# Linear attention's state updates as single fp32 products of unsplit keys and values, in one burst of alternating row halves

## The chip, the core and the metric

The kernel runs on one core of a Trainium2 chip. The core has a matrix engine (TensorE, here PE; its weight loads are listed as PEld), a vector engine (VectorE, DVE), a scalar engine (ScalarE, ACT), GpSimd (POOL) and SyncE (SP). SP and POOL issue most of the DMAs. Each engine works through its own queue in program order and waits on semaphores that the others raise. The metric is the device time of one execution, in microseconds; the figures quoted are medians of several runs, and the profile is of one more execution.

## The reference, cut to what matters

Two layers of a hybrid encoder, over 512 frames of width 2048. In each layer one input projection feeds a gated linear attention (GLA) with four heads and a chunked softmax attention with eight; both are normalised, gated, concatenated and mapped by one output projection. The change is in the linear attention, in its state updates `U`:

```
def gla_chunk_causal(q, k, v, log_a):
    ...
    L = jnp.cumsum(log_a.astype(jnp.float32).reshape(B, nc, CHUNK, H, DK), axis=2)
    L_end = L[:, :, -1]
    k_dec = kf * jnp.exp(L_end[:, :, None] - L)
    U = jnp.einsum('bnchk,bnchv->bnhkv', k_dec, vf)
    A = jnp.exp(L_end)
    def step(state, inp):
        a, u = inp
        new = a[..., None] * state + u
        return new, new
    ...
    o = jnp.einsum('bnchk,bnhkv->bnchv', qf, states)
```

A chunk is 64 frames, there are eight of them; a head's keys are 128 wide (DK) and its values 256 (DV). So `U` is, for each of the four heads and eight chunks, a product of a 64 x 128 by a 64 x 256 matrix: the 64 frames are the rows of the array that are summed over, and the result is 128 x 256.

## The kernel before

**Precision.** The large projections are computed from split operands: a value x is stored as a rounded part hi (type fp32r) and the rest lo = x - hi, and a product is the sum of three fp32r products, hi·hi, hi·lo and lo·hi. `split` (L107) makes hi with a cast on ACT (L108) and lo with a subtraction on DVE (L109); `split_scaled` (L111) does the same with a factor (L112, L113). Some smaller products use fp32 operands as they are: the attention's mixing (L920), transposes, and the reading of the GLA states (L1124).

**The main stream.** `std_gemm` (products at L341) and `fast_gemm` (L417 with features as rows, L427 otherwise) run through the weight blocks in a fixed list of jobs. For each job SP fetches a 512 KB block (`raw` or `H`, L156), ACT casts its hi part (`wh`, L218), DVE makes its lo part (`wl`, L223), and PE multiplies. Blocks are prepared some jobs ahead, in rings of four buffers (`wl`: three). Beside this stream, generators in a list `tasks` are advanced by `pump` after each job (`Pace`), so that the products of the attention heads, the GLA heads and the like stand between main products. The order in which each engine's queue is written is then settled by a scheduler that simulates the program; it can put main products into the middle of what the code writes as one group.

**The GLA part of a layer.** After the softmax heads, `fast_gemm` with the block pair GK, GQ calls `kq_consume` for each of four token tiles of keys and of queries. A key tile is multiplied by its decay and split into `kdh` and `kdl` (slots g8, g11, g14, g15). The pair GV0, GV1 calls `gv_consume`: value tiles are split into `gvh` and `gvl`, one pair of slots for each j (two heads) and each half of the frames p. When both halves of a j are there, `gla_heads` is started: it makes a `Unit` for each of two heads and two halves of the frames, eight units a layer. A unit does

- `outer` (products at L1090): for each of its four chunks (tile tt, half cc of the tile's 128 rows) the three products kh·vh, kh·vl, kl·vh, 64 rows by 256 columns, into `ps_u[cc]`, a PSUM bank of the pool of four that all `ax` tiles share. That is 12 products a unit. The half cc = 0 lies on the array's rows 0 to 63, cc = 1 on rows 64 to 127;
- `states` (L1109, L1111): four steps on DVE, each chunk's state from the one before and `ps_u`;
- `read` (L1124): four fp32 products of the queries with the states, each to one half (64 columns) of the array;
- `norm`, `gate`, and later `turn` (transposes at L1152, and the result's split and its store `fg`, L1167).

After the two GV blocks come the output projection's blocks (`std_gemm`, L341). `output_sums` loads pieces of the heads' results (`fa`, L655, and `fg`, L659), adds and splits them and stores sums (L629), and token rows of x are loaded on POOL's queue (L497), behind the last norm.

Of the kernel before, what the change touches and what calls it, by code (L numbers as in the profile page):

```python
# [8 lines left out]
F32R = mybir.dt.float32r  # L9
# [25 lines left out]
def hybrid_trunk(  # L35
# [674 lines left out]
    def layer(l):  # L710
# [319 lines left out]
        kdh, kdl, gqT = [], [], []  # L1030
# [13 lines left out]
        def kq_consume(j, h, t, src, comb):  # L1044
            z = settled(src, comb)
            if j:
                if not gqT:
                    until(lambda: 6 in heads_done)
                    gqT.extend(slot(tag, [2, 512]) for tag in ("g12", "g13"))
                tasks.insert(0, transpose_q(2 * h + t, z))  # L1050
                return
            if not kdh:
# [17 lines left out]
        class Unit:  # L1070
            def __init__(self, h, p, gvh, gvl, prev):
                self.h, self.p, self.gvh, self.gvl = h, p, gvh, gvl
                self.st = slot(f"g{9 + p}", [4, 256])
                self.prev = prev.st[:, 3, :] if p else None

            def outer(self):
# [4 lines left out]
                for tt in range(2):  # L1081
                    ops = []
                    for cc in range(2):
                        r = slice(cc * 64, (cc + 1) * 64)
                        kh, kl = kdh[p][r, tt, hk], kdl[p][r, tt, hk]
                        vh, vl = self.gvh[p][r, tt, hv], self.gvl[p][r, tt, hv]
                        ops.append(((kh, vh), (kh, vl), (kl, vh)))
                    for i in range(3):
                        for cc in range(2):
                            nc.tensor.matmul(  # L1090
                                self.ps_u[cc][:, tt * 256 : (tt + 1) * 256], ops[cc][i][0], ops[cc][i][1],
                                start=(i == 0), stop=(i == 2),
                            )
# [77 lines left out]
        def gla_heads(j, gvh, gvl):  # L1171
            units = []

            def new(k):
                h, p = 2 * j + k // 2, k % 2
                units.append(Unit(h, p, gvh, gvl, units[-1] if p else None))
                units[-1].outer()
# [30 lines left out]
        gvh, gvl = {}, {}  # L1208
        GV = {1: ("g4", "g5", "g6", "g7"), 0: ("g0", "g1", "g2", "g3")}
# [16 lines left out]
        def gv_consume(j, h, t, src, comb):  # L1226
            z = settled(src, comb)
            if (j, h) not in gvh:
                until(lambda: 4 in heads_done)
                gvh[j, h] = slot(GV[j][h], [2, 512], F32R)  # L1230
                gvl[j, h] = slot(GV[j][2 + h], [2, 512], F32R)
            if comb is None:
                split_scaled(gvh[j, h][:, t, :], gvl[j, h][:, t, :], src, inv_rms(l, 2 * h + t))
            else:
                split(gvh[j, h][:, t, :], gvl[j, h][:, t, :], z)
            if h and t:
                heads = gla_heads(j, [gvh[j, p] for p in range(2)], [gvl[j, p] for p in range(2)])
# [172 lines left out]
```

## Time and profile before

| what | value |
|---|---|
| median of 3 runs | 1637.59 us (1635.76 to 1638.52) |
| the profiled execution, its own time | 1637.15 us |
| its span, first to last instruction | 1635.2 us |
| mean granted TensorE clock | 0.999 |
| HBM, read and written | 395.83 MB and 71.06 MB, 286 GB/s over the span |
| weight blocks, SP, 512 KB each | 319 + 56, median 5.8 and 5.2 us from issue to landing |

In a list of instruction groups each row has line, engine, operation, what is written from what, shapes, count, then busy time in us, mean duration of one in ns, and the engine's idle time just before them with what ended it. In the timeline a row is start and duration in us and what ran, neighbours of one kind merged with their count. A matmul's duration holds the time until its results are out, so that the next starts before its end: what a product costs in a stream is read from start to start. A layer's GLA units stand at about 593 to 673 us of the span in the first layer and 1407 to 1487 us in the second.

### The profile page before, as it was taken

The numbers are of one execution on the slowest core, as the hardware profiler recorded it, in microseconds if no ns is written. First come the engines' busy times: TensorE is split into PE (matmuls) and PEld (weight loads), VectorE is DVE, ScalarE is ACT, GpSimd is POOL, SyncE is SP. The second block draws the span as 40 slices with busy tenths as digits, with TensorE's granted clock in tenths as the row PEclk, the third lists the DMA queues.
The fourth block names the chain that finished last, engine by engine and source line by source line (L and its number), as shares of the span: only waits on it lengthen the run. The fifth ranks groups of instructions, "written<-read, shape, count | busy, mean of one in ns | idle before, by whom it ended". The sixth has DMA issues, their size and how long they took to land.

```text
span 1635.2 us, 24844 instructions
## 1 busy us (share of the span) xinstructions
PE 1625.8 (99%) x8990; PEld 1392.6 (85%) x8990; DVE 1228.0 (75%) x1587; ACT 904.6 (55%) x1516; POOL 169.9 (10%) x259
## 2 busy tenths in 40 slices
PE   9999999999999999999999999999999999999998
PEld 7888889999978877788888888899999888777886
DVE  7567776877877886778886676768778778866887
ACT  8444544556676644555783445445566665445553
POOL 1210000001101201310122000000001012013100
PEclk9999999999999999999999999999999999999999
DMA  9979786858868696898789697968588676969986
GB/s 374 360 280 322 283 313 227 304 181 311 291 196 283 208 378 233 308 364 315 276 303 388 228 332 268 321 221 304 187 312 274 218 265 232 355 225 332 376 307 233
DMA packets 150778, 469.59 MB, mean 287 GB/s; under 512 B 16428, under 2 KB 35892, under 8 KB 150656
## 3 DMA queue, kind: packets, MB, share of 16 engines
q1 hardware_dynamic: 128064, 389.69, 68.1%
q0 software_dynamic: 22016, 77.37, 12.0%
q8 instruction: 71, 1.16, 0.3%
q10 hardware_dynamic: 576, 0.95, 0.2%
q14 instruction: 51, 0.42, 0.1%
HBM read 395.83 MB, written 71.06 MB: 286 GB/s over the span
## 4 chain that ended last, share of the span: by engine, by line
PE 99%; DMA 0%; DVE 0%; ACT 0%; SPq 0%; DVEq 0%; POOLq 0%; issue 0%
PE mm L427 46%; PE mm L341 22%; PE mm L417 20%; PE ax L920 2%; PE ax L1090 1%; PE ax L427 1%; PE ax L903 1%; PE ax L1124 1%; PE ax L745 1%; PE ax L882 1%; PE ax L883 1%; PE ax L881 1%; PE ax L1152 0%; PE ax L569 0%; PE ax L951 0%; DMA raw<-in_w_dram 0%
## 5 line engine op out<-in xcount | busy, mean ns | idle before, releaser
L427 PE MATMUL mm<-wh,sa 128*128 128x512 f32 x1536 | 485.1, 391 | 0.0
L218 ACT CAST wh<-raw 128x1024 fp32r<-128x1024 f32 x255 | 269.1, 1057 | 255.7 <-PE mm L427 115.8
L223 DVE TENSOR_TENSOR wl<-raw,wh 128x1024 fp32r<-128x1024 f32 (+1 forms) x257 | 312.3, 1217 | 125.5 <-PE mm L427 44.1
L218 ACT CAST wh<-H 128x1024 fp32r<-128x1024 f32 x224 | 235.3, 1053 | 217.6 <-PE mm L427 109.9
L223 DVE TENSOR_TENSOR wl<-H,wh 128x1024 fp32r<-128x1024 f32 x224 | 273.1, 1222 | 106.6 <-PE mm L427 46.4
L427 PEld LDWEIGHTS mm<-wh,sa 128*128 128x128 f32 x1536 | 287.9, 188 | 62.2 <-issue 1.5
L427 PE MATMUL mm<-wl,sa 128*128 128x512 f32 x768 | 299.9, 390 | 0.0
L417 PE MATMUL mm<-sa,wh 128*128 128x256 f32 x1280 | 237.3, 286 | 0.0
L417 PEld LDWEIGHTS mm<-sa,wh 128*128 128x128 f32 x1280 | 199.9, 191 | 0.3
L427 PE MATMUL mm<-wh,a 128*128 128x512 f32 x576 | 185.7, 393 | 0.0
L417 PE MATMUL mm<-sa,wl 128*128 128x256 f32 x640 | 180.6, 283 | 0.0
L427 PEld LDWEIGHTS mm<-wl,sa 128*128 128x128 f32 x768 | 144.3, 188 | 30.3
L341 PE MATMUL mm<-wh,a 128*128 128x512 f32 x512 | 167.4, 394 | 0.1
L207 DVE TENSOR_TENSOR H<-H,raw 128x1024 f32<-128x1024 f32 x120 | 145.9, 1220 | 3.5 <-DMA raw<-in_w_dram 1.8
L465 POOL TENSOR_TENSOR sm<-sm,mhalf 128x4 f32<-128x4 f32 (+2 forms) x40 | 60.6, 1514 | 777.7 <-DVE sm L936 550.8
L427 PEld LDWEIGHTS mm<-wh,a 128*128 128x128 f32 x576 | 107.9, 188 | 23.2 <-issue 0.8
L417 PEld LDWEIGHTS mm<-sa,wl 128*128 128x128 f32 x640 | 122.3, 191 | 0.1
L341 PEld LDWEIGHTS mm<-wh,a 128*128 128x128 f32 x512 | 96.0, 188 | 21.1 <-ACT wh L215 0.5
L427 PE MATMUL mm<-wl,a 128*128 128x512 f32 x288 | 113.0, 392 | 0.0
L341 PE MATMUL mm<-wl,a 128*128 128x512 f32 x256 | 100.1, 392 | 0.0
L417 PE MATMUL mm<-a,wh 128*128 128x256 f32 x512 | 94.9, 285 | 0.0
L341 PE MATMUL mm<-wh,sa 128*128 128x512 f32 x256 | 85.9, 394 | 0.0
(208 smaller groups left out, 2332.9 us busy)
## 6 DMA issues: line engine op xcount, KB each, us to landing
raw<-in_w_dram SPq DMA_DIRECT2D x319, 512.0 KB, 5.8
sa<-S SPq DMA_DIRECT2D x192, 512.0 KB, 4.7
H<-in_w_dram SPq DMA_DIRECT2D x56, 512.0 KB, 5.2
sa<-A SPq DMA_DIRECT2D x48, 512.0 KB, 6.1
S<-g POOLq DMA_DIRECT2D x32, 512.0 KB, 7.6
oS<-g POOLq DMA_DIRECT2D x32, 512.0 KB, 6.3
sa<-oS SPq DMA_DIRECT2D x32, 512.0 KB, 5.2
sg<-t POOLq DMA_DIRECT2D x32, 256.0 KB, 6.1
```

The lines of the kernel that those rows point to most:

```text
L207: nc.vector.tensor_tensor(out=h, in0=h, in1=r, op=ALU.add)
L218: last_cast[0] = nc.scalar.copy(self.wh, src).ins
L223: last_low[0] = nc.vector.tensor_tensor(out=self.wl[:, kk, :], in0=self.src[:, kk, :], in1=self.wh[:, kk, :].bitcast(F32), op=ALU.subtract ...
L341: mm = nc.tensor.matmul(pss[o], a[:, part, t], rhs[:, kk, :], start=(i == 0 and kk == 0 and m == 0), stop=(i == n - 1 and kk == 1 and m == 2),
L417: nc.tensor.matmul(dst, lhs[:, kk, f], a[:, part, tok], start=(fresh and kk == 0 and m == 0 and ft % 2 == 0), stop=(c == c_last and kk == ...
L427: nc.tensor.matmul(out_ps[t], a[:, part, tok], rhs[:, kk, :], start=(fresh and kk == 0 and m == 0), stop=(c == c_last and kk == 1 and m == ...
L465: return nc.gpsimd.tensor_tensor(out=out_r, in0=v, in1=mhalf[:, : v.shape[-1]], op=ALU.pow).ins
L745: nc.tensor.matmul(ps[0:96, half * 256 : (half + 1) * 256], wga[kt // 10][:, kt % 10, :], op[:, i, (kt % 2) * 256 : (kt % 2 + 1) * 256], s ...
L881: nc.tensor.matmul(ps[:, :n], self.qh[:, t], self.kh[:, :n], start=True, stop=False)
L882: nc.tensor.matmul(ps[:, :n], self.qh[:, t], self.kl[:, :n], start=False, stop=False)
L883: nc.tensor.matmul(ps[:, :n], self.ql[:, t], self.kh[:, :n], start=False, stop=True)
L920: nc.tensor.matmul(o, self.pt[i][:, j * P : (j + 1) * P], av[hd // 4, j // 2][:, j % 2, (hd % 4) * P : (hd % 4 + 1) * P], start=(j == 0), ...
```

## The change

Keys and values are no longer split: `kq_consume` writes the decayed keys into fp32 slots `kd`, `gv_consume` writes the values into fp32 slots `gv`, and `outer` makes one fp32 product for each chunk where it made three fp32r ones. The four products of a unit alternate between the row halves (cc = 1, 0, 1, 0), each with an edge to the one before, so that the scheduler keeps their order. A one-column memset on DVE of `ps_u[0]` stands before them. The slots g14, g15, g6, g7, g2 and g3 are no longer used for this. `Unit`, `gla_heads` and their callers take `gv` in place of `gvh` and `gvl`.

```
         def kq_consume(j, h, t, src, comb):
-            z = settled(src, comb)
             if j:
+                z = settled(src, comb)
...
-                kdh.extend(slot(tag, [2, 512], F32R) for tag in ("g8", "g11"))
-                kdl.extend(slot(tag, [2, 512], F32R) for tag in ("g14", "g15"))
+                kd.extend(slot(tag, [2, 512]) for tag in ("g8", "g11"))
+            dst = kd[h][:, t, :]
             if comb is None:
-                kd, z = z, t2()
                 nc.vector.scalar_tensor_tensor(
-                    out=z, in0=kd, scalar=inv_rms(l, 2 * h + t), in1=decay[h][:, t, :], op0=ALU.mult, op1=ALU.mult
+                    out=dst, in0=src, scalar=inv_rms(l, 2 * h + t), in1=decay[h][:, t, :], op0=ALU.mult, op1=ALU.mult
                 )
             else:
-                nc.vector.tensor_tensor(out=z, in0=z, in1=decay[h][:, t, :], op=ALU.mult)
-            split(kdh[h][:, t, :], kdl[h][:, t, :], z)
+                z = settled(src, comb)
+                nc.vector.tensor_tensor(out=dst, in0=z, in1=decay[h][:, t, :], op=ALU.mult)
...
                 self.ps_u = [aux(), aux()]
-                for tt in range(2):
-                    ops = []
-                    for cc in range(2):
+                nc.vector.memset(self.ps_u[0][:, 0:1], 0.0)
+                mm = None
+                for tt in (1, 0):
+                    for cc in (1, 0):
                         r = slice(cc * 64, (cc + 1) * 64)
-                        kh, kl = kdh[p][r, tt, hk], kdl[p][r, tt, hk]
-                        vh, vl = self.gvh[p][r, tt, hv], self.gvl[p][r, tt, hv]
-                        ops.append(((kh, vh), (kh, vl), (kl, vh)))
-                    for i in range(3):
-                        for cc in range(2):
-                            nc.tensor.matmul(
-                                self.ps_u[cc][:, tt * 256 : (tt + 1) * 256], ops[cc][i][0], ops[cc][i][1],
-                                start=(i == 0), stop=(i == 2),
-                            )
+                        with tc.issue_after(mm) if mm else nullcontext():
+                            mm = nc.tensor.matmul(
+                                self.ps_u[cc][:, tt * 256 : (tt + 1) * 256], kd[p][r, tt, hk], self.gv[p][r, tt, hv],
+                                start=True, stop=True,
+                            ).ins
...
-        GV = {1: ("g4", "g5", "g6", "g7"), 0: ("g0", "g1", "g2", "g3")}
+        GV = {1: ("g4", "g5"), 0: ("g0", "g1")}
...
-            z = settled(src, comb)
-            if (j, h) not in gvh:
+            if (j, h) not in gv:
                 until(lambda: 4 in heads_done)
-                gvh[j, h] = slot(GV[j][h], [2, 512], F32R)
-                gvl[j, h] = slot(GV[j][2 + h], [2, 512], F32R)
+                gv[j, h] = slot(GV[j][h], [2, 512])
+            dst = gv[j, h][:, t, :]
             if comb is None:
-                split_scaled(gvh[j, h][:, t, :], gvl[j, h][:, t, :], src, inv_rms(l, 2 * h + t))
+                nc.scalar.activation(dst, src, AF.Copy, scale=inv_rms(l, 2 * h + t))
             else:
-                split(gvh[j, h][:, t, :], gvl[j, h][:, t, :], z)
+                comb(dst)
```

In the changed program the line numbers past the new code are smaller by four: the outer products are L1086 (before L1090), the reads L1120 (before L1124), the memset is L1080.

Where these products stand in PE's queue is settled by the scheduler. The rows below are a place in the first layer, of the third unit (head 3, first half of the frames), before the change. A row is line, operation, what it writes from what (with the buffers' numbers) and the shape; `ax_6307` and `ax_6308` are the two banks `ps_u[0]` and `ps_u[1]`, that is the two row halves, and `ax_6321` is the read of the unit before. The six products of the other half (`ax_6307`) stand six main products earlier, in a row too.

```order
L427 MATMUL mm_5724<-wl_6205,a_55_470 128x512
L1090 MATMUL ax_6308<-g_1142_6092,g_1028_5572 128x256
L1090 MATMUL ax_6308<-g_1143_6093,g_1028_5572 128x256
L1090 MATMUL ax_6308<-g_1142_6092,g_1030_5574 128x256
L1090 MATMUL ax_6308<-g_1142_6092,g_1028_5572 128x256
L1090 MATMUL ax_6308<-g_1143_6093,g_1028_5572 128x256
L1090 MATMUL ax_6308<-g_1142_6092,g_1030_5574 128x256
L1124 MATMUL ax_6321<-g_1172_6233,g_977_5335 64x256 x4
L427 MATMUL mm_5724<-wh_6179,a_55_470 128x512
```

The same unit in the changed program; `ax_6267` and `ax_6268` are its two banks.

```order
L427 MATMUL mm_5712<-wl_6179,a_55_470 128x512
L1086 MATMUL ax_6268<-g_1137_6078,g_1027_5570 128x256
L1086 MATMUL ax_6267<-g_1137_6078,g_1027_5570 128x256
L1086 MATMUL ax_6268<-g_1137_6078,g_1027_5570 128x256
L1086 MATMUL ax_6267<-g_1137_6078,g_1027_5570 128x256
L1120 MATMUL ax_6274<-g_1162_6200,g_977_5335 64x256 x4
L427 MATMUL mm_5712<-wh_6160,a_55_470 128x512
```

A layer's 96 outer products in 17 groups, some of both halves, some of one half alone, become 32 in eight groups of four, each alternating. Groups of outer products and of reads that stand directly side by side are five a layer before and four after; one read that was in two pieces is in one.

SP's queue changes too. This is a place about 100 us after a layer's GLA units begin, in the first layer before the change: weight fetches (L156), and the loads of heads' results for the output sums (L655, L659).

```order
L156 DMA raw_7142<-in_w_dram 128x1024
L655 DMA t_1395_7226<-fa_173 128x2x256
L156 DMA raw_7165<-in_w_dram 128x1024
L156 DMA raw_7295<-in_w_dram 128x1024
L659 DMA t_1396_7227<-fg_181 128x512
L156 DMA raw_7329<-in_w_dram 128x1024
```

And the same place in the changed program.

```order
L156 DMA raw_7050<-in_w_dram 128x1024
L655 DMA t_1381_7134<-fa_173 128x2x256
L659 DMA t_1382_7135<-fg_181 128x512
L156 DMA raw_7073<-in_w_dram 128x1024
L156 DMA raw_7203<-in_w_dram 128x1024
L655 DMA t_1383_7136<-fa_173 128x2x256
```

The load L659 has moved ahead of two weight fetches. It waits until the store of `fg` that used its buffer before has landed (on the first layer's timeline, the store issued by POOL at 692.34 us).

More of the change, by code (lines that the diff above doesn't have):

```diff
@@ L1169, in turn, with gla_heads @@
                 og[p, h] = op
-        def gla_heads(j, gvh, gvl):
+        def gla_heads(j, gv):
             units = []
@@ L1226, in gv_consume @@
         def gv_consume(j, h, t, src, comb):
[L1227 to L1228 removed]
+            if (j, h) not in gv:
                 until(lambda: 4 in heads_done)
[L1230 to L1231 removed]
+                gv[j, h] = slot(GV[j][h], [2, 512])
+            dst = gv[j, h][:, t, :]
             if comb is None:
[L1233 removed]
+                nc.scalar.activation(dst, src, AF.Copy, scale=inv_rms(l, 2 * h + t))
             else:
[L1235 removed]
+                comb(dst)
             if h and t:
[L1237 removed]
+                heads = gla_heads(j, [gv[j, p] for p in range(2)])
                 tasks.append(heads if j else beside(heads, early_sums(), 3))
```

12 lines of the change are left out of this document (6 added, 6 removed).

## The prediction

> **What bounds the kernel now.** The page comes first: the span, the busy shares and the chain that ended last.
>
> ```profile
> span 1635.2 us, 24844 instructions
> PE 1625.8 (99%) x8990; PEld 1392.6 (85%) x8990; DVE 1228.0 (75%) x1587; ACT 904.6 (55%) x1516; POOL 169.9 (10%) x259
> PE 99%; DMA 0%; DVE 0%; ACT 0%; SPq 0%; DVEq 0%; POOLq 0%; issue 0%
> ```
>
> The matrix engine is the chain, so the end moves by what the change does to PE's own sequence, and by any wait it puts into it. A busy PE is not yet a PE at its peak, so next I read the two lines concerned (shortest, median and longest ns of a weight load and of a product, then rows*columns of the array), and the list of what the weight loads wait for.
>
> ```profile
> L1090 PEld LDWEIGHTS ax<-g,g x192: 182/184/188, 593.3 to 1478.1; 64*128 64x128 f32 x192
> L1090 PE MATMUL ax<-g,g x192: 271/278/386, 593.3 to 1478.2; 64*128 64x256 f32 x192
> ...
> L1124 PEld LDWEIGHTS ax<-g,g x128: 132/136/137, 610.5 to 1487.1; 128*64 128x64 f32 x128
> L1124 PE MATMUL ax<-g,g x128: 379/379/430, 610.5 to 1487.3; 128*64 128x256 f32 x128
> ...
> PEld ax L1090 <- issue: 8.1, 24, 0.4
> ```
>
> L1090 is the outer products (64 rows of the array), L1124 the state reads (64 columns). The program has 64 reads and the trace 128 records: an unsplit fp32 product runs as two records. The fp32r products of L1090 have one each. In 24 places the weight loader stands 0.34 us (8.1/24) in front of an outer product for nothing that the profile shows. To see why, I went through the timeline at such places; columns are start and duration in us, then what ran.
>
> ```profile
> 592.79 0.39 PE L427 MATMUL mm<-wl,sa 128*128 128x512 f32 x1
> 593.01 0.39 PE L427 MATMUL mm<-wh,sa 128*128 128x512 f32 x1
> 593.33 0.38 PE L1090 MATMUL ax<-g,g 64*128 64x256 f32 x2
> 593.65 0.49 PE L427 MATMUL mm<-wh,sa 128*128 128x512 f32 x1
> 593.98 0.39 PE L427 MATMUL mm<-wl,sa 128*128 128x512 f32 x1
> ...
> 625.12 0.39 PE L427 MATMUL mm<-wh,sa 128*128 128x512 f32 x1
> 625.43 0.97 PE L1090 MATMUL ax<-g,g 64*128 64x256 f32 x6
> 626.33 0.50 PE L427 MATMUL mm<-wh,sa 128*128 128x512 f32 x1
> 626.67 0.40 PE L427 MATMUL mm<-wl,sa 128*128 128x512 f32 x1
> ...
> 663.14 0.39 PE L341 MATMUL mm<-wl,a 128*128 128x512 f32 x1
> 663.46 0.99 PE L1090 MATMUL ax<-g,g 64*128 64x256 f32 x12
> 664.38 0.50 PE L341 MATMUL mm<-wh,a 128*128 128x512 f32 x1
> 664.71 0.39 PE L341 MATMUL mm<-wh,sa 128*128 128x512 f32 x1
> ```
>
> Start to start, main products follow each other every 0.22 to 0.23 us (I use 0.227). Into the burst the step is 0.32, out of it 0.32, and the first step after it 0.33. So every excursion from full-array products to row halves and back has a fixed price, which I call the switch. An excursion costs (next main start less last main start less 0.227) + (first step after it less 0.227):
> - 2 products, one on each half: 0.64 - 0.227 + 0.33 - 0.227 = 0.52.
> - 6 products, all on one half (the order shown with the change tells which): 1.21 + 0.34 - 0.454 = 1.10.
> - 12 products, 6 on each half: 1.24 + 0.33 - 0.454 = 1.12.
>
> Twelve cost what six do: **the two row halves run side by side**, and they did although the order issues four of one half, then four of the other. What counts is the slots, the products on the fuller half: 0.40 + 0.117 per slot (from 0.52 at one and 1.10 at six).
>
> **The change part by part.** *PE, removed.* Following L1090 through order and timeline, a layer has 17 excursions with 1, 2, 1, 3, 1, 5, 6, 6, 6, 6, 1, 6, 6, 6, 6, 6, 6 slots, 74 together. Standing alone they cost 17 x 0.40 + 74 x 0.117 = 15.5 us. The eight reads stand in nine excursions; one whole read, and one that touches a burst:
>
> ```profile
> 633.36 0.40 PE L427 MATMUL mm<-wl,sa 128*128 128x512 f32 x1
> 633.69 1.08 PE L1124 MATMUL ax<-g,g 128*64 128x256 f32 x8
> 634.70 0.50 PE L427 MATMUL mm<-wh,sa 128*128 128x512 f32 x1
> 635.04 0.40 PE L341 MATMUL mm<-wh,a 128*128 128x512 f32 x1
> ...
> 616.12 0.40 PE L427 MATMUL mm<-wl,a 128*128 128x512 f32 x1
> 616.45 0.97 PE L1090 MATMUL ax<-g,g 64*128 64x256 f32 x6
> 617.36 1.08 PE L1124 MATMUL ax<-g,g 128*64 128x256 f32 x8
> 618.37 0.50 PE L427 MATMUL mm<-wh,a 128*128 128x512 f32 x1
> 618.71 0.40 PE L427 MATMUL mm<-wh,sa 128*128 128x512 f32 x1
> ```
>
> A read costs 1.34 + 0.34 - 0.454 = 1.23. Together with the burst it is 2.25 + 0.34 - 0.454 = 2.14, against 1.10 + 1.23 = 2.33 apart: a join saves 0.19. The ninth excursion, one product of a split read, I put at 0.8 (a read less half its 0.7 of later slots). Reads: 8 x 1.23 + 0.8 = 10.6; the order joins five times, -0.95. Before: 15.5 + 10.6 - 0.95 = 25.1 us a layer.
>
> *PE, added.* A new burst has four fp32 products, two on each row half, two records each: four slots a half. No row shows a 64-row fp32 product. The nearest is the read, which also has four fp32 products of 256 columns, on two column halves: its eight records take 1.08, the last alone 0.38 (379 ns), so 0.70 for the three slots before it, some 0.21 to 0.27 each. Hence the read's 1.23, plus 0.05 because the first weight load, which nothing hides, brings 128 columns and not 64 (medians 184 and 136 ns): 1.28. Bounds: 1.10, the six fp32r slots, and 1.28 + 4 x 0.21 = 2.12 with no overlap; I take 1.28, the read being the same arithmetic. After: 8 x 1.28 + 8 x 1.23 - 4 joins x 0.19 = 19.3 a layer. **Saved: 2 x (25.1 - 19.3) = 11.6 us.** All other products are the same in number and shape.
>
> A sentence apart: the Trainium skill, FP8 and Floating Point Precision, "TensorE Precision Notes", gives true FP32 four passes through the array, so one product would stream more than the three it replaces (64 x 4 against 192 passes of 256 columns), and as an estimate, at half of the read's 0.21 us slot for a pass and with no overlap on either side, the change would lose 64 x 0.105 = 6.7 us. The trace agrees with the passes (a read's record lasts 0.10 longer than an fp32r product of as many columns, and there are two) and adds the overlap and the switches, which that count leaves out.
>
> *DVE and ACT.* The splits go: ten casts on ACT and twelve vector operations on DVE a layer. Eight memsets come.
>
> ```profile
> L109 DVE TENSOR_TENSOR g<-t,g 128x512 fp32r<-128x512 f32 x12 | 8.2, 685 | 0.1
> L223 DVE TENSOR_TENSOR wl<-raw,wh 128x1024 fp32r<-128x1024 f32 x16 | 19.6, 1223 | 9.0 <-PE mm L341 3.9 <-PE mm L427 3.6 <-ACT t L1134 1.0
> L862 DVE MEMSET bias<- 64x64 f32 x16 | 1.8, 112 | 6.2 <-DMA bias<-in_rel_dram 6.1
> ```
>
> These are DVE groups (the first two from 580 to 670 us alone, the third from the whole run): count, busy time, mean ns, idle before. Freed on DVE: about 12 x 0.69 = 8.2 us a layer; the memset of a column costs at most the 0.11 of a wider one. I price both at nothing for the end, since PE covers them. The new wait is the point: in four of a layer's eight bursts, by the order with its waits, the second product waits for DVE, with all main products queued behind it. Bounds: 0, and one L223 ahead of each memset, 16 x 1.22 = 19.6 us. I take 0, because here DVE idles 9.0 us before its L223, mostly for PE: it runs ahead.
>
> *What is late next.* PE reaches the stage after the heads 5.8 us earlier in each layer. That stage is fed by DMA. The stretches first (their last two figures are the DMA engines' share and GB/s), then the timeline:
>
> ```profile
> 655.00:660.00 5.00, 5.00 (x28) 3.51 (x28) 4.12 (x10) 0.82 (x2) 0.71 (x1) 1.00 0.01 4
> 700.00:710.00 10.00, 10.00 (x46) 8.06 (x44) 5.25 (x8) 3.37 (x6) 0.54 (x1) 1.00 1.04 402
> ```
>
> ```profile
> 709.93 0.19 PEld L341 LDWEIGHTS mm<-wl,a 128*128 128x128 f32 x1 [0.31 <-DVE wl L223]
> ...
> 692.34 0.55 POOL L1167 DMA_DIRECT2D fg<-t  x1 [0.83 <-DMA g<-in_x_dram]
> 698.70 1.69 SPq L156 DMA_DIRECT2D raw<-in_w_dram  x2
> 703.65 0.33 SPq L659 DMA_DIRECT2D t<-fg  x1
> ```
>
> DMA is idle from 655, full from 700, and at 709.9 a weight load already waits. What fills the DMA engines (sums, stores, token rows) is released by the heads, so it starts earlier too, from an idle gap: I let it move along. But SP's order changes: L659, which went out at 703.65 behind two weight fetches (698.70), now stands ahead of both, and it waits for the store issued at 692.34. Then two 512 KB fetches can leave up to 5.0 us later. Bounds: 0, and 5.0 us a layer. As the engines stay full meanwhile, what is lost is nearer to the 256 KB that now go first, 0.65 us at 402 GB/s: I take 0.75 a layer, **1.5 us**.
>
> The sum: 1637.15 (the profiled execution: span 1635.2 and 1.95 around it) - 11.6 + 1.5 = **1627.1 us**. That execution is 0.4 below the median of the runs, 1637.59, inside their spread.
>
> **The rivals.**
> - *No overlap in fp32 (the other side).* If 64-row fp32 products hold the whole array, each burst has four slots more: 16 x 4 x 0.21 = 13.4, and 1627.1 + 13.4 = 1640.5, slower. It decides from three extra slots of four on (10.1 / 16 / 0.21). For it: no row has this shape. Against: 663.46 and 633.69 overlap with either half kind.
> - *Loads not hidden inside a half.* Each later slot then costs an exposed load, 0.10 (at 625.43, 0.97 less one product's 0.28 leaves 0.69 for five steps; four at 0.117 leave 0.22 for the first, the one with its load exposed): 16 x 3 x 0.10 = 4.8, 1631.9. Against: those four steps. The Trainium skill, TensorE: Matmul & The Clock Gate, "Part 3: Packing small matmuls — row/col tiling", says loads overlap running products only where the row group differs; by that rule this rival holds, and those four steps at 0.117 disagree.
> - *The later stage keeps its clock times.* If the fetches behind 709.93 stay DMA-bound where they are, PE waits there for what it won: half of it gives 1632.9, all of it 1637, no change. For: DMA full at 700, SP's new order. Against: the idle gap at 655.
> - *The memset holds PE.* At half its bound, 9.8 us, 1637.
>
> **How the numbers follow.** Forecast 0.70 (1624.5 to 1629.5); loads not hidden 0.08; later stage 0.10, half of it near 1633; no overlap 0.08; memset 0.04. A range of 1623.5 to 1634 takes in the first two and half the third, 0.83. A measurement of this kernel tells 0.2%, 3.3 us, from no change. Faster (below 1634.3): 0.70 + 0.08 + 0.05 = 0.83. Within: 0.05 + 0.02 + half of no overlap 0.04 = 0.11. Slower: 0.06.
>
> **What would show it.** Right: eight excursions of L1086 a layer, eight records each, as pairs in four slots, about 1.4 us from main start to main start. Records spaced 0.21 one by one mean no overlap; 0.32 a slot, loads not hidden. A wait of PEld on L1086 from DVE shows the memset; one of L341 near 704 us, above 0.3, the DMA stage. I am wrong if the bursts are as said and PE waits several us a layer elsewhere.

## The result, and the profile after

| | before | after |
|---|---|---|
| median of 6 runs | 1637.79 us (1635.76 to 1638.52) | 1624.85 us (1624.06 to 1625.54) |
| the profiled execution | 1637.15 us | 1624.06 us |
| weight loads and products on PE | 8990 each | 8926 each |

The ratio is 0.9922, with a 95% interval from 0.9909 to 0.9935: faster by 12.9 us. The forecast was 1627.1, with a range of 1623.5 to 1634.0.

The page of the changed kernel, the lines that answer to the first three shown of before:

```profile
span 1622.3 us, 24662 instructions
PE 1612.9 (99%) x8926; PEld 1385.0 (85%) x8926; DVE 1215.1 (75%) x1579; ACT 895.1 (55%) x1496; POOL 162.6 (10%) x259
PE 99%; DVE 0%; ACT 0%; DVEq 0%; POOLq 0%; issue 0%
```

PE is the whole chain in both kernels, and it is 12.9 us shorter. The two lines concerned (shortest, median and longest ns), and then a row on what the weight loads wait for:

```profile
L1086 PEld LDWEIGHTS ax<-g,g x128: 182/186/187, 600.7 to 1466.0; 64*128 64x128 f32 x128
L1086 PE MATMUL ax<-g,g x128: 376/376/480, 600.7 to 1466.2; 64*128 64x256 f32 x128
...
L1120 PE MATMUL ax<-g,g x128: 379/379/431, 607.8 to 1473.4; 128*64 128x256 f32 x128
```

```profile
PEld ax L1086 <- issue: 3.2, 10, 0.4
```

A unit's four products are eight records (64 products, 128 records), as the reads' were. Both kinds now last as long as each other, 376 and 379 ns. The weight loader's stops of some 0.3 us in front of outer products that are put down to nothing else are down from 24 to 10. The timeline of one burst alone and one joined to a read:

```profile
600.34 0.39 PE L427 MATMUL mm<-wh,a 128*128 128x512 f32 x1
600.66 1.13 PE L1086 MATMUL ax<-g,g 64*128 64x256 f32 x8
601.72 0.50 PE L427 MATMUL mm<-wh,a 128*128 128x512 f32 x1
602.06 0.40 PE L427 MATMUL mm<-wl,a 128*128 128x512 f32 x1
...
612.12 0.39 PE L427 MATMUL mm<-wl,a 128*128 128x512 f32 x1
612.44 1.13 PE L1086 MATMUL ax<-g,g 64*128 64x256 f32 x8
613.51 1.08 PE L1120 MATMUL ax<-g,g 128*64 128x256 f32 x8
614.52 0.50 PE L427 MATMUL mm<-wh,a 128*128 128x512 f32 x1
```

Alone, a burst costs (601.72 - 600.34) + (602.06 - 601.72) - 0.454 = 1.27 us. Joined, (614.52 - 612.12) + 0.34 - 0.454 = 2.29, 0.2 less than a burst and a read apart. Such sums over every place of the two layers' linear attention where small products of any kind stand between main products (outer products, reads, and the transposes, which the prediction did not count and whose number is the same) come to 57.5 us before and 45.8 after: **11.7 us less**.

A second measure is used below: how far one kernel's n-th main product (L341, L417, L427; 7584 in every trace) starts ahead of the other's. The changed kernel is 0.81 us ahead at product 2801, before the first layer's linear attention, and 6.93 at product 3421, behind it and the first block of the output projection; in the second layer it goes from 6.88 (6701) to 12.87 (7201). That is 6.1 and 6.0 us, once in each layer, and nothing in between. The first 0.8 us is not the change's: it is there by product 50, 18 us into the run, where the other kernels' traces stand between 0.5 us behind and 0.9 ahead of the kernel before. So 12.1 of the 12.9 us between these two executions belong to the change.

The later stage, in the windows (the last two figures are the DMA engines' share and GB/s) and in the timeline of POOL's and SP's DMA issues:

```profile
655.00:660.00 5.00, 5.00 (x30) 3.35 (x29) 3.82 (x8) 2.60 (x5) 1.71 (x3) 1.00 1.01 330
...
700.00:710.00 10.00, 10.00 (x46) 8.28 (x45) 8.14 (x10) 6.66 (x10) 1.60 (x3) 1.00 1.03 412
```

```profile
670.87 3.20 POOL L497 DMA_DIRECT2D g<-in_x_dram  x6
...
693.20 0.32 SPq L659 DMA_DIRECT2D t<-fg  x1
693.61 0.86 SPq L156 DMA_DIRECT2D raw<-in_w_dram  x2
```

The idle gap of the DMA engines at 655 us (share 0.01 before) is gone. L659 stands ahead of two fetches now, as the order said, but the fetches leave at 693.61 and 694.09, where they left at 698.70 and 700.06 before. PE is 6.7 us earlier in this stage, so against PE they leave 1.6 and 0.7 us later. The token rows of x, first sent at 680.08 before, go out at 670.87:

```profile
680.08 1.07 POOL L497 DMA_DIRECT2D g<-in_x_dram  x2
```

No wait of PE or of its weight loads stands there (none between 690 and 730 us): the stop at 709.93 is gone.

### The profile page after: what moved, and what is told of

Same layout as the page of the kernel before. It is cut to its first block, busy times and chain, and to the rows that moved or that the text cites. A ratio compares the mean times of both kernels' runs of the same rounds, so it can differ in the third digit from the quotient of the medians.

```text
span 1622.3 us, 24662 instructions
## 1 busy us (share of the span) xinstructions
PE 1612.9 (99%) x8926; PEld 1385.0 (85%) x8926; DVE 1215.1 (75%) x1579; ACT 895.1 (55%) x1496; POOL 162.6 (10%) x259
## 3 DMA queue, kind: packets, MB, share of 16 engines
q0 software_dynamic: 22016, 77.37, 12.2%
q8 instruction: 71, 1.16, 0.3%
## 4 chain that ended last, share of the span: by engine, by line
PE 99%; DVE 0%; ACT 0%; DVEq 0%; POOLq 0%; issue 0%
PE mm L427 46%; PE mm L341 22%; PE mm L417 20%; PE ax L920 2%; PE ax L427 1%; PE ax L903 1%; PE ax L1086 1%; PE ax L1120 1%; PE ax L745 1%; PE ax L882 1%; PE ax L883 1%; PE ax L881 1%; PE ax L569 0%; PE ax L951 0%; PE ax L1148 0%; PE ax L674 0%
## 5 line engine op out<-in xcount | busy, mean ns | idle before, releaser
L427 PE MATMUL mm<-wh,sa 128*128 128x512 f32 x1536 | 484.3, 391 | 0.0
L223 DVE TENSOR_TENSOR wl<-raw,wh 128x1024 fp32r<-128x1024 f32 (+1 forms) x257 | 312.2, 1216 | 126.2 <-PE mm L427 43.0
L223 DVE TENSOR_TENSOR wl<-H,wh 128x1024 fp32r<-128x1024 f32 x224 | 273.3, 1222 | 109.6 <-PE mm L427 49.0
L427 PEld LDWEIGHTS mm<-wh,sa 128*128 128x128 f32 x1536 | 287.7, 188 | 61.6 <-issue 1.5
L427 PE MATMUL mm<-wl,sa 128*128 128x512 f32 x768 | 299.6, 390 | 0.0
L417 PE MATMUL mm<-sa,wh 128*128 128x256 f32 x1280 | 237.3, 286 | 0.0
L417 PEld LDWEIGHTS mm<-sa,wh 128*128 128x128 f32 x1280 | 199.9, 191 | 0.3
L427 PE MATMUL mm<-wh,a 128*128 128x512 f32 x576 | 186.1, 393 | 0.0
L417 PE MATMUL mm<-sa,wl 128*128 128x256 f32 x640 | 180.6, 283 | 0.0
L427 PEld LDWEIGHTS mm<-wl,sa 128*128 128x128 f32 x768 | 144.2, 188 | 30.3
L341 PE MATMUL mm<-wh,a 128*128 128x512 f32 x512 | 166.5, 393 | 0.0
L465 POOL TENSOR_TENSOR sm<-sm,mhalf 128x4 f32<-128x4 f32 (+2 forms) x40 | 53.6, 1340 | 779.9 <-DVE sm L936 544.9
L427 PEld LDWEIGHTS mm<-wh,a 128*128 128x128 f32 x576 | 107.9, 188 | 24.8 <-issue 2.9
L417 PEld LDWEIGHTS mm<-sa,wl 128*128 128x128 f32 x640 | 122.3, 191 | 0.1
L341 PEld LDWEIGHTS mm<-wh,a 128*128 128x128 f32 x512 | 96.1, 188 | 20.9 <-issue 0.8
L427 PE MATMUL mm<-wl,a 128*128 128x512 f32 x288 | 112.3, 390 | 0.0
L341 PE MATMUL mm<-wl,a 128*128 128x512 f32 x256 | 100.6, 394 | 0.0
L417 PE MATMUL mm<-a,wh 128*128 128x256 f32 x512 | 94.9, 285 | 0.0
L341 PE MATMUL mm<-wh,sa 128*128 128x512 f32 x256 | 85.7, 394 | 0.0
```

Source lines behind the costliest of these rows:

```text
L223: last_low[0] = nc.vector.tensor_tensor(out=self.wl[:, kk, :], in0=self.src[:, kk, :], in1=self.wh[:, kk, :].bitcast(F32), op=ALU.subtract ...
L341: mm = nc.tensor.matmul(pss[o], a[:, part, t], rhs[:, kk, :], start=(i == 0 and kk == 0 and m == 0), stop=(i == n - 1 and kk == 1 and m == 2),
L417: nc.tensor.matmul(dst, lhs[:, kk, f], a[:, part, tok], start=(fresh and kk == 0 and m == 0 and ft % 2 == 0), stop=(c == c_last and kk == ...
L427: nc.tensor.matmul(out_ps[t], a[:, part, tok], rhs[:, kk, :], start=(fresh and kk == 0 and m == 0), stop=(c == c_last and kk == 1 and m == ...
L465: return nc.gpsimd.tensor_tensor(out=out_r, in0=v, in1=mhalf[:, : v.shape[-1]], op=ALU.pow).ins
```

## The experiments

The theory that the first three test: PE's time in this stage is set by excursions out of the full array and by the slots in them. Its main rival: the gain comes from having fewer products, or from the splits that DVE and ACT no longer do. Every run is set against before in its own comparison (medians 1636.6 to 1636.8 there), and against the changed kernel's 1624.85.

**The burst alone, with the splits kept.** The kernel before, only `outer` written in the new manner:

```
+                nc.vector.memset(self.ps_u[0][:, 0:1], 0.0)
+                mm = None
+                for tt in (1, 0):
...
                     for i in range(3):
-                        for cc in range(2):
+                        for cc in (1, 0):
+                            with tc.issue_after(mm) if mm else nullcontext():
+                                mm = nc.tensor.matmul(
```

> The kernel before, with its splits and its 96 fp32r products a layer, and only the new order: alternating halves, an edge from product to product, the memset ahead. The scheduler then makes 13 excursions with outer products a layer (1, 2, 3, 1, 5, 6, 1, 6, 6, 6, 6, 1, 6 slots, 50 together), and six reads stand directly behind a burst. Theory (excursions and slots set the time): 13 x 0.40 + 50 x 0.117 + 8 x 1.23 - 6 x 0.19 = 19.7 us a layer, against 25.1 in the kernel before and 19.3 in the changed one: 1625.7 us (1624 to 1628), level with the changed kernel although nothing is taken from DVE or ACT. Rival (the gain comes from fewer products, or from the splits that went): close to the kernel before, 1634 to 1638.

Measured: 1626.01 us (1625.9 to 1626.63), ratio 0.9935 (0.9922 to 0.9947). One of its bursts, 12 fp32r products, with a read joined behind it (four transposes follow):

```profile
615.59 0.39 PE L427 MATMUL mm<-wl,sa 128*128 128x512 f32 x1
615.90 0.97 PE L1093 MATMUL ax<-g,g 64*128 64x256 f32 x12
616.81 1.08 PE L1127 MATMUL ax<-g,g 128*64 128x256 f32 x8
```

It gained 5.5 us on the kernel before in each layer's linear attention (the theory's 25.1 - 19.7 is 5.4), with all 192 fp32r products and all splits in place. Grouping makes the gain; fp32, fewer products and the relief of DVE and ACT are not needed for it, but for the 1.16 us between this kernel and the changed one.

**The fp32 products without the memset.**

```
-                nc.vector.memset(self.ps_u[0][:, 0:1], 0.0)
```

> The changed kernel without the memset. The four fp32 products of a unit are then taken apart by the scheduler, mostly into one and three with main products between, and reads into three and one: 18 excursions a layer in place of 12. Theory (excursions): with 0.45 + 0.21 a slot for an fp32 excursion and 1.23 for a read they come to 25.3 us a layer against 19.3, so 12 us more than the changed kernel, 1636.8 us (1633 to 1638), though it has no splits and the same products. Rivals: the memset held PE, then faster than the changed kernel, 1620 to 1624; the gain was DVE's and ACT's relief, then level with the changed kernel, 1624 to 1626.

Measured: 1635.76 us (1635.05 to 1636.84), ratio 0.9995 (0.9986 to 1.0004): no change from before. The timeline shows a unit taken apart, its first product alone and the other three later:

```profile
610.45 0.40 PE L427 MATMUL mm<-wh,a 128*128 128x512 f32 x1
610.77 0.70 PE L1085 MATMUL ax<-g,g 64*128 64x256 f32 x2
611.40 0.50 PE L427 MATMUL mm<-wh,a 128*128 128x512 f32 x1
...
613.35 0.39 PE L427 MATMUL mm<-wh,a 128*128 128x512 f32 x1
613.66 1.13 PE L1085 MATMUL ax<-g,g 64*128 64x256 f32 x6
```

Three products (six records) take the 1.13 us of four. One memset of 59 ns a unit is worth 10.9 us: with it the burst stays whole. It writes one of the unit's two banks; how the scheduler gets from that to whole bursts, no run shows.

**Without memset and edges.**

```
-                nc.vector.memset(self.ps_u[0][:, 0:1], 0.0)
-                mm = None
-                for tt in (1, 0):
-                    for cc in (1, 0):
+                for tt in range(2):
+                    for cc in range(2):
...
-                        with tc.issue_after(mm) if mm else nullcontext():
```

> The changed kernel without the memset and without the edges, the products in the order tile 0 both halves, tile 1 both halves. The scheduler makes the same twelve excursions a layer as in the changed kernel. Theory (excursions): as the changed kernel, 1624.9 us, within 1 us. Rival (memset holds PE, or the edges do): faster by 2 us or more.

Measured: 1634.02 us (1633.01 to 1635.23), ratio 0.9984 (0.9975 to 0.9992). The expectation was wrong about the order: in the trace there are 36 groups of outer products and reads, not 24, many of them two products of one unit. The time is that of the greater count, so the miss speaks for the excursions; the rival, faster by 2 us, did not come.

**Half after half.**

```
-                for tt in (1, 0):
-                    for cc in (1, 0):
+                for cc in (1, 0):
+                    for tt in (1, 0):
```

> The changed kernel with the four products in another order: both of the upper row half, then both of the lower, with the edges kept. Theory (each row half takes its own stream, whatever the order, as the splits' bursts of four and four showed): the same burst, 1.38 us from main start to main start, and the same time within 1 us. Rival (the halves overlap only as neighbours in the order): the second product of a half waits behind the first, two to three slots of 0.21 more a burst, 16 x 0.42 to 0.63 = 7 to 10 us more.

Measured: 1624.72 us (1624.52 to 1625.93). A burst of its timeline:

```profile
600.79 0.39 PE L427 MATMUL mm<-wh,a 128*128 128x512 f32 x1
601.11 1.14 PE L1086 MATMUL ax<-g,g 64*128 64x256 f32 x8
602.18 0.50 PE L427 MATMUL mm<-wh,a 128*128 128x512 f32 x1
```

1.39 us from main start to main start, against 1.38. In a burst of four products, the alternation of halves is worth nothing; the two halves run side by side in either order.

**All on one half.**

```
-                        r = slice(cc * 64, (cc + 1) * 64)
+                        r = slice(64, 128)
```

> The changed kernel with all four products on the upper row half; it leaves out the lower half's keys and values and takes the upper half's twice. This is the price of no overlap. Theory: eight slots in place of four, 16 x 4 x 0.21 = 13.4 us more than the changed kernel, 1638.3 us (1636 to 1641). If loads inside a half are hidden, records stand 0.21 apart; if each load of a half is exposed, 0.32 apart and 16 x (8 x 0.32 - 4 x 0.21) = 27 us more. Rival (the overlap is worth nothing): no more than 2 us.

Measured: 1638.35 us (1637.54 to 1639.71), 13.5 us more than the changed kernel.

```profile
600.88 0.39 PE L427 MATMUL mm<-wh,a 128*128 128x512 f32 x1
601.20 1.99 PE L1086 MATMUL ax<-g,g 64*128 64x256 f32 x8
603.12 0.50 PE L427 MATMUL mm<-wh,a 128*128 128x512 f32 x1
```

The same eight records take 2.24 us from main start to main start, 0.86 more: four slots at 0.215. This is the price of the prediction's rival "no overlap in fp32", and it would have made the change worthless. At 0.215 a record with a weight load of 0.186 in front of each, loads inside one half are hidden too.

Over the kernels in which PE does not wait in the later stage, the sum of all excursions, counted as for the result, goes with the time of the profiled execution:

| kernel | excursions, us | time, us |
|---|---|---|
| changed | 45.8 | 1624.06 |
| half after half | 45.9 | 1624.52 |
| burst with splits | 46.4 | 1626.63 |
| without memset and edges | 54.4 | 1633.33 |
| without memset | 57.0 | 1635.76 |
| before | 57.5 | 1637.15 |
| all on one half | 59.5 | 1639.71 |

Time less excursions stays within 2.0 us, from 1578.3 to 1580.3.

**The splits put back beside the fp32 products.** After each key and value tile:

```
+            spare = slot(("g14", "g15")[h], [2, 512], F32R)
+            split(spare[:, 0, :], spare[:, 1, :], dst)
```

> The changed kernel with the splits put back beside the fp32 slots: each key and value tile is cast on ACT and subtracted on DVE into slots that nothing reads, twelve of each a layer. The scheduler makes 15 excursions a layer instead of 12. Theory (DVE's and ACT's relief is worth nothing by itself): only the three excursions, 0.87 + 0.8 + 0.19 a layer, 3.7 us in all: 1628.6 us (1627 to 1630). Rival (the relief is the gain, or a part): what stands over these 3.7 us, up to 1638.

Measured: 1649.51 us (1646.62 to 1651.43), ratio 1.0073 (1.006 to 1.0086): 21 us more than expected. The excursions are those expected, 42.56 us of them with the transposes that stand in them, against 38.98 in the changed kernel. The rest is in the later stage. The timeline at that place:

```profile
705.50 0.39 PE L341 MATMUL mm<-wh,a 128*128 128x512 f32 x1
...
708.16 1.04 ACT L218 CAST wh<-raw 128x1024 fp32r<-128x1024 f32 x1 [0.91 <-DMA raw<-in_w_dram]
...
709.26 1.22 PE L341 MATMUL mm<-wh,a 128*128 128x512 f32 x2 [3.37 <-ACT wh L218]
710.52 0.80 PE L341 MATMUL mm<-wl,a 128*128 128x512 f32 x1
711.11 1.05 PE L341 MATMUL mm<-wh,a 128*128 128x512 f32 x2
711.97 0.63 PE L341 MATMUL mm<-wl,a 128*128 128x512 f32 x1
712.39 0.63 PE L341 MATMUL mm<-wh,a 128*128 128x512 f32 x1
```

PE waits for a cast, the cast for a weight block; and behind the wait the products follow each other every 0.42 us in place of 0.227. It is the stage for which the prediction had its +1.5. So the rival had a point that the theory lacked: the work on DVE and ACT does matter here, and the timeline suggests that it does so by what it puts off. The next runs separate the two engines.

**ACT's half, DVE's half.** The same tiles, once with a cast alone, once with a subtraction alone:

```
+            nc.scalar.copy(spare[:, t, :], dst)
```

```
+            nc.vector.tensor_tensor(out=spare[:, t, :], in0=dst, in1=dst, op=ALU.subtract)
```

> The changed kernel with only ACT's half of the splits put back: twelve casts a layer of key and value tiles into slots that nothing reads. The order has 14 excursions a layer (one join less, one read in three and one), by the prices measured so far 0.19 + 0.78 more a layer, 2 us in all: 1626.8 us if PE never waits. Theory A (the work put on DVE holds up the heads' results, and with them the sums, stores and token rows that fill the DMA engines, so that a weight block comes late near 709 us and PE waits): no such wait here, 1626 to 1628. Theory B (ACT's casts do it): a wait of 2 us or more near 709 us in each layer, 1638 or more.

> The changed kernel with only DVE's half: twelve subtractions a layer, 0.69 us each, of a key or value tile from itself, into slots that nothing reads. The order has 16 excursions a layer, by the prices measured so far 2.6 us a layer more, 5.2 us in all: 1630 us if PE never waits. Theory A (DVE's work delays what fills the DMA engines): a wait of 2 us or more near 709 us in each layer and a slowed stretch behind it, 1640 us or more, token loads on POOL from about 680 us and not 671. Theory B (ACT's casts): no such wait, 1629 to 1631.

Measured: 1637.28 us (1635.67 to 1640.36) with the casts and 1636.67 us (1633.32 to 1639.2) with the subtractions; both ratios span 1. The wait is in both, 2.3 us at 706.79 and 1.9 at 707.55, so neither theory alone holds, and the times fall short of the 1638 and 1640 that they gave. What the two have in common is the landing of weight blocks. DMA issues between 685 and 705 us (KB each, median us from issue to landing), first before, then changed, then with the casts. The trace tells the landing of few of these blocks: of one, four and two of them.

```profile
raw<-in_w_dram SPq DMA_DIRECT2D x5, 512.0 KB, 12.2
```

```profile
raw<-in_w_dram SPq DMA_DIRECT2D x6, 512.0 KB, 8.0
```

```profile
raw<-in_w_dram SPq DMA_DIRECT2D x4, 512.0 KB, 13.4
```

**Token rows later.** The kernel with all splits back, the loads of x written after the next projection block:

```
-        with tc.issue_after(last_norm[0]):
-            xs0 = load_tokens(0, x_src, nc.gpsimd)
...
         std_gemm(l, NB_IN + 1, (0, 1), OO, operand_out, out_evac(1), rate=0.6, lag=2)
+        with tc.issue_after(last_norm[0]):
+            xs0 = load_tokens(0, x_src, nc.gpsimd)
```

> The kernel with the splits put back (1649.5 us, PE waiting 3.8 us for a cast at 709 us and 3.5 us at 1530 us, each with a slowed stretch behind it), and the 4 MB of token rows loaded after the next 32 main jobs of the output projection instead of before them. Theory (PE waits because the weight blocks share the DMA engines with these loads): the two waits and the slowed stretches go, 14 to 18 us less, 1631 to 1636. Rival (PE waits because ACT or DVE come late with the cast itself): the waits stay, 1645 to 1650.

Measured: 1648.4 us (1647.83 to 1651.46). The edit did not do what it says: the scheduler sent the token rows at 681.28 us, where they had gone at 680.95. The run tells nothing either way.

**Token rows earlier.** The kernel with ACT's casts, without the edge:

```
-        with tc.issue_after(last_norm[0]):
-            xs0 = load_tokens(0, x_src, nc.gpsimd)
-            xs1 = load_tokens(1, x_src, nc.gpsimd)
+        xs0 = load_tokens(0, x_src, nc.gpsimd)
+        xs1 = load_tokens(1, x_src, nc.gpsimd)
```

> The kernel with ACT's half of the splits put back (1637.3 us, a wait of 2.7 and 2.5 us near 707 and 1522 us with slowed products behind each), with the same products in the same order on PE, and one edge taken away: the token rows of x may be loaded as soon as their buffers are free, not only behind the last norm, so they go out in part before and among the heads' stores. Theory (PE waits there because the weight blocks come late through DMA engines that these loads fill): the waits and the slowed stretches go and about 10 us with them, 1626.8 us (1625.5 to 1629). Rival (the casts themselves, or SP's wait for the store ahead of the fetches, hold the blocks up): the waits stay, 1635 to 1638.

Measured: 1630.18 us (1629.44 to 1631.07), ratio 0.9963 (0.9949 to 0.9976). The loads go out from 593.8 us on, and the weight blocks land in less than half the time. Their row between 685 and 705 us, then what PE waits for (us in total, times, longest), the first row being that of the start:

```profile
raw<-in_w_dram SPq DMA_DIRECT2D x5, 512.0 KB, 5.7
```

```profile
PE ax L674 <- DVE t L671: 1.2, 1, 1.2
PE mm L427 <- DVE wl L223: 1.1, 2, 0.5
PE mm L341 <- DVE a L109: 0.8, 2, 0.4
```

The wait near 707 and the slowed products are gone, with the same casts in place; 7.1 of the 10.5 us that were expected come back. PE's order is not quite the expected one (one read a layer and some transposes moved), but its excursions sum to the same within 0.1 us. The 3.4 that don't are in part the waits on L223 and L109, 1.9 us. With ACT's casts, then, what makes PE wait in this stage is DMA, and it is the token rows that fill it. For DVE's subtractions the same was not run.

**The heads' results loaded on POOL's queue.**

```
-                nc.sync.dma_start(tiles[2 * half + 1], of_gla[l][half, c])
+                nc.gpsimd.dma_start(tiles[2 * half + 1], of_gla[l][half, c])
```

> The changed kernel with the loads of the linear attention's results for the output sums on POOL's queue instead of SP's, so that no weight fetch stands behind their wait for the store. This takes away the whole of what was priced at 1.5 us. Theory now (the term is nothing, since the stage moved along as a whole and its fetches have slack): the same as the changed kernel within 1 us. Rival (the order on SP does cost, and something else paid for it): 1 to 2 us faster.

Measured: 1626.0 us (1625.84 to 1628.91), 1.15 more than the changed kernel, so a little outside the "within 1 us", and on the other side of the rival. Nothing is won in all by freeing SP of L659's wait. The run does not isolate it, though: POOL's queue, which now carries these loads, sends the token rows at 675.99 and not 670.87, and a small gain on SP may be lost again by that.

**Whole split bursts, reads joined.** The attempt at a faster kernel, with one-column copies ahead of the burst, and:

```
+                nc.vector.tensor_copy(self.ps_u[1][:, 0:1], self.gvl[p][:, 1, 0:1].bitcast(F32))
+                nc.vector.tensor_copy(self.ps_u[1][:, 0:1], kdl[p][:, 1, 0:1].bitcast(F32))
...
+                if k < 3:
+                    new(k + 1)
+                    last = units[k + 1].last
+                units[k].read(last)
```

> The split kernel with each unit's 12 fp32r products in one whole burst (three one-column writes ahead of it, two of which read the last split operands, so that it starts when all is there) and a read called directly behind the next unit's burst: 8 bursts of six slots and nine read excursions a layer, six of them joined to a burst. Theory (excursions): 8 x 1.10 + 8 x 1.23 + 0.8 - 6 x 0.19 = 18.3 us a layer, 2 us less than the changed kernel in all: 1622.8 us (1621 to 1625), with three times the products and all the splits. Rival (fewer products or splits): 1634 or more. If the burst has to wait for its operands at PE, a wait on DVE at the outer products shows it.

Measured: 1639.51 us (1637.14 to 1641.25), ratio 1.0015 (1.0007 to 1.0024). That is 16.7 us more than expected, and inside the rival's range. The excursions came as planned (a whole burst 1.10 to 1.12, with a read 2.01 to 2.13), so it is not the number of products that costs; waits do, by the list of PE's waits:

```profile
PE ax L1160 <- DVE sg L1150: 5.1, 2, 2.9
PE mm L427 <- DVE wl L223: 1.7, 1, 1.7
PE mm L341 <- ACT wh L218: 1.6, 1, 1.6
```

Reads that come later make `gate` (L1150) late for `turn` (L1160), and the token rows go at 681.08: the same stage again. No kernel of the study is measurably faster than the changed one.

**The later stage in one table.** The first token load on POOL; the start of main product 3301 (near the end of the output projection's first block); the weight blocks' median landing between 685 and 705 us (of one to four blocks each); and by how much longer than in the changed kernel PE takes from product 3301 to 3421. All are of the profiled executions; those with ACT's half and with whole split bursts took 1640.36 and 1641.25 us, 3.1 and 1.7 more than their medians.

| kernel | token rows sent | product 3301 | between | blocks land in | lost |
|---|---|---|---|---|---|
| before | 680.08 | 701.27 | 21.2 | 12.2 | 0.22 |
| changed | 670.87 | 694.56 | 23.7 | 8.0 | 0.00 |
| burst with splits | 673.75 | 696.18 | 22.4 | 9.7 | 0.32 |
| without memset | 677.07 | 700.94 | 23.9 | 8.1 | 0.00 |
| without memset and edges | 676.37 | 699.68 | 23.3 | 8.0 | 0.00 |
| half after half | 670.62 | 695.07 | 24.5 | 7.8 | 0.00 |
| all on one half | 677.06 | 701.96 | 24.9 | 8.2 | 0.00 |
| heads' loads on POOL | 675.99 | 695.11 | 19.1 | 6.6 | 0.78 |
| ACT's half | 676.64 | 696.13 | 19.5 | 13.4 | 6.11 |
| DVE's half | 679.01 | 697.37 | 18.4 | 15.3 | 4.20 |
| whole split bursts | 681.08 | 698.59 | 17.5 | 14.0 | 5.21 |
| splits back | 680.95 | 697.57 | 16.6 | 15.2 | 6.76 |
| ACT's half, rows early | from 593.77 | 697.06 | 103 | 5.7 | 0.00 |

In these traces, blocks that land in 10 us or less cost less than 1 us; at 13 to 15 us PE loses 4 to 7 us in this layer. The kernel before, at 12.2 us by one block, stood just short of that edge. The loss does not go with the time at which the rows leave (none at 677.06, 6.11 at 676.64) but, roughly, with the time left from there to product 3301: 21 us or more in the kernels that lose next to nothing, 16.6 to 19.5 in those that lose 4 us or more; the heads' loads on POOL, with 19.1 and 0.78, fit neither.

Two pairs of rows tell what sent the token rows 9.2 us earlier. The new order alone (burst with splits against before) brings 6.3 us; no splits and fp32 products without the whole bursts (without memset against before) bring 3.0, though PE gains only 0.3 us up to product 3301 there. Together that is 9.3.

## Why the prediction was right, and where it was off

- **The switch and the slots: right.** 11.6 us were forecast for PE's own sequence; the excursions fell by 11.7 us, and the lead grew by 6.1 and 6.0. A burst was put at 1.28 and is 1.27, a join at 0.19 and is 0.2. The price, worked out from fp32r bursts and reads of before, held in kernels that mix them otherwise: 1625.7 expected and 1626.01 measured with the splits, 1636.8 and 1635.76 without the memset.
- **Overlap of the row halves in fp32: right.** It was the step without a row of its own. Eight records on two halves take 1.38 us between main products, on one half 2.24; the rival's 13.4 us were priced well (13.5), and it did not happen.
- **Loads hidden inside a half: right**, by the 0.215 us steps of the run on one half.
- **The memset at nothing: right.** Sixteen of 59 ns, and no wait of PE on one. Its use was not seen: without it the burst comes apart and the time goes back to 1635.76.
- **The later stage, +1.5: the mis-sized term; it measured 0, or 0.2 gained.** The step was "I let it move along", with 0.75 us a layer for L659 ahead of two fetches. The fetches do leave later against PE, by 1.6 and 0.7 us, so the delay was rightly seen. But the stage did not merely move along: PE reached it 6.7 us earlier, its token rows went out 9.2 us earlier, and the blocks landed in 8.0 us and not 12.2, so that no wait of PE came of it. Of the 2.25 us between forecast and median this is 1.5; the other 0.75 lies inside the spread of the runs before, 2.8 us.
- **DVE and ACT at nothing, "since PE covers them": right for their own time, not as a rule.** Putting back ACT's half costs 12.4 us, of which the two more groups a layer account for some 2. Most of the rest goes when the token rows are sent early, with the casts still there. So ACT's added work acts through the time at which the heads' results release the DMA traffic. The prediction looked at this stage and its DMA, but not at this link. In the changed kernel the relief of both engines counts for about 3 of the 9.2 us, by the two pairs above; the rest is the new order. The relief was not needed here: the burst with all splits lost only 0.32 us in this stage.

The rival of the later stage, given 0.10, was the right place to fear: the kernels on the wrong side of that edge lose there up to about what the excursions won.

## What to carry to other kernels

Small products that use a part of the array should stand together, with as many as possible between two full-array products, and something (an edge, a shared bank, a one-column write) must keep a scheduler from taking them apart; here the price was about 0.4 us for each trip and the slots of the fuller half, whatever the number of products. When work off the critical engine is removed or added, look at what its results release: the DMA traffic behind it, and how much slack the critical engine's own fetches have when that traffic meets them. A stage in which a weight load already waits, as for 0.31 us at 709.93 before, is an edge: ask on which side of it the change puts the kernel.

## What the runs showed of the hardware

- **A wait of 2 to 4 us can cost as much again.** In the kernel with ACT's casts PE waited from 704.07 to 706.79, start to start; the products behind it come like this:

```profile
709.75 0.63 PE L341 MATMUL mm<-wl,a 128*128 128x512 f32 x1
710.18 0.63 PE L341 MATMUL mm<-wh,a 128*128 128x512 f32 x1
710.60 0.63 PE L341 MATMUL mm<-wl,a 128*128 128x512 f32 x1
```

  Every 0.427 us in place of 0.227, until about 713, and the granted clock of the windows is 0.83 (the column ahead of the DMA share):

```profile
700.00:710.00 10.00, 7.37 (x26) 5.27 (x25) 6.21 (x9) 5.03 (x7) 1.33 (x3) 0.83 1.04 409
710.00:720.00 10.00, 10.00 (x38) 8.05 (x38) 7.47 (x9) 5.97 (x10) 0.81 (x2) 0.83 0.94 342
```

  Of the 6.1 us lost there, some 2.5 are the wait, 0.7 a second one at 708.31, and the rest slow products. Gaps of 2.0 us from start to start and more were followed by slow products, but for one of 2.1 us (at 746.91 with whole split bursts); single gaps of 1.6 us (at 749.70 with the splits back) were not, but one of 1.4 and one of 1.2 us close together were (at 1521.48 and 1523.05 with DVE's half). The slow stretches last some 2 to 6.5 us. The Trainium skill, TensorE: Matmul & The Clock Gate, "Part 1: The HAM clock gate (the "warmup" mystery)", has the array at half clock after an idle window of about 3.4 us, and back at full clock after as long a busy one; by its figure a cold product of 512 columns takes 426.7 ns. The trace agrees with the rate, and with the slow stretch in its order of size only. It differs in the trigger: gaps of 2.7 and 2.5 us from start to start, and once of 2.0, were enough here.
- **Order inside a burst does not matter for the two row halves.** Half after half and alternating halves both give 1.38 to 1.39 us for eight records, and with half after half, too, the records start in four pairs, 0.013 us apart (from 601.11 us on). So the second half's stream starts while the first half's later products still wait.
